# S5 chunk recurrence in two levels, and layer 0's readout with the states as stationary operand, in a two-layer hybrid diffusion block

## The chip, the core and the metric

One core of a Trainium2 chip runs the whole program in one launch. The metric is the device time of one execution in microseconds; the kernel is compared by the median of its runs. In the rows, PE is TensorE (matmul), PEld its weight loads, DVE is VectorE, ACT is ScalarE, POOL is GpSimd, SP is the engine whose queue issues most DMAs. L652 is line 652 of the kernel before.

## The reference

Two layers over 512 latent tokens and 256 context tokens, width 1024. Each layer normalizes, projects the input into three branches (a bidirectional S5 state space model, a gated DeltaNet, windowed attention), merges them by gates and adds an MLP. The change is in the S5 branch: for each of 32 groups, 64 complex states and two directions,

```python
s_re, s_im = associative_scan(complex_affine_combine, (a_re, a_im, bu_re, bu_im), reverse=reverse)
y = y + einsum('blgp,ghp->blgh', s_re, c_re) - einsum('blgp,ghp->blgh', s_im, c_im)
```

that is s[t] = a s[t-1] + B u[t], first over the context tokens and then over the latent ones from the state that the context left, forwards and backwards. The last layer has no context output.

## The kernel before

Tokens are cut into chunks of 8: 32 context chunks (NCC) and 64 latent ones (NCL), 96 in all (NCH). Within a chunk the S5 is a set of products with tables that depend on the weights alone; only the state at the chunks' borders needs a recurrence.

`s5_in` (L608) does two things. For each of 16 pairs of groups (pr), TensorE multiplies the chunk inputs u4 with a table om (L631) and ScalarE and VectorE copy the result into the state tile st, shifted by one chunk (L634 to L637). Then the recurrence runs over the chunks in place, both directions at once: 94 steps of four products and sums on VectorE (L652 to L655), each over 128 partitions x 64 elements (2 directions, real and imaginary, 16 pairs). Each step needs the one before.

`s5_out` (L659) reads the states out: for each pair a product with u4 (L678, L685) and four with the tables gm (L680, L690). In layer 0 (with_ctx) the tables are the stationary operand, 128 columns, and the 96 chunks move; the output has the right layout at once. In layer 1 the latent chunks' states are stationary, 64 columns, the table of 128 columns moves, two halves lie on different quarters of the array, and four transposes (L703) per quarter of the readout turn the result. Both write yt and then DRAM.

The program is written as Python generators; a scheduler puts the instructions of each engine into a fixed order when the program is built, and each engine runs its own order. Around the recurrence stand, in both layers, twelve convolutions of the DeltaNet inputs (`dn_conv`): a weight group is loaded (ws), split into a high and a low part (wh on ScalarE L227; wl on VectorE, or on GpSimd in these stretches, L228), TensorE multiplies (L178, into pg), ScalarE copies into cxp (L867), VectorE and GpSimd add the taps (L876, L880) and VectorE writes the result (L888). cxp, cac and ctp have two buffers each. The attention's k and q pass through the same buffers and a rotation (L731 to L734) and splits (L749, L775). In layer 0 the readout is drawn in between attention units (L797 to L844), which take their transposes' PSUM from the same two banks (tag "s") as the readout; in layer 1 it precedes the DeltaNet's main part, whose gaps are filled with the gates' products (L178).

```python
    for k in range(1, NCH - 1):
        v.tensor_tensor(t1, view(k - 1), A12[:, 0], op=OP.mult)
        v.tensor_tensor(t2, view(k - 1, True), A12[:, 1], op=OP.mult)
        v.tensor_tensor(t1, t1, view(k), op=OP.add)
        v.tensor_tensor(view(k), t1, t2, op=OP.add)
```

Of the kernel before, what the change touches and what calls it, by code (L numbers as in the profile page):

```python
# [607 lines left out]
def s5_in(g, l, pool, u4):  # L608
    nc = g.nc
    st = g.st = pool.tile([128, 2, 2, 16, SLOT], F32, name="st")  # L610
    nc.gpsimd.memset(st[:, 0, :, :, 0], 0.0)
    nc.gpsimd.memset(st[:, 1, :, :, NCC - 1], 0.0)
    A12 = pool.tile([128, 2, 2, 2, 16], F32, name="A12")
    v = nc.vector
    for d in range(2):
        s = slice(l * 32 + d * 16, l * 32 + d * 16 + 16)
        ar, ai = g.apw[:, 0, s, 7], g.apw[:, 1, s, 7]
        v.tensor_copy(A12[:, 0, d, 0], ar)
        v.tensor_copy(A12[:, 0, d, 1], ar)
        v.tensor_scalar(A12[:, 1, d, 0], ai, -1.0, None, op0=OP.mult)  # L620
        v.tensor_copy(A12[:, 1, d, 1], ai)
    tb = g.tb[l]
    for pr in range(16):
# [14 lines left out]
    RS = 16 * SLOT  # L638
    DS = 2 * RS

    order = list(range(NCC - 1, -1, -1)) + list(range(NCH - 1, NCC, -1))
    rpos = [(c - 1) % NCH for c in order]

    def view(k, swap=False):
        f, r = k + 1, rpos[k]
        dd = [[DS + r - f, 2], [-RS if swap else RS, 2], [SLOT, 16]]
        return raw(st, f + (RS if swap else 0), dd)

    for k in range(1, NCH - 1):
        t1 = pool.tile([128, 2, 2, 16], F32, name="rt1", tag="rt1", bufs=2)  # L650
        t2 = pool.tile([128, 2, 2, 16], F32, name="rt2", tag="rt2", bufs=2)
# [7 lines left out]
def s5_out(g, l, pool, upool, u4, with_ctx, yd):  # L659
# [3 lines left out]
    n = NCH - c0  # L663
    for m in range(4):
        mt = pool.tile([128, 8, 128], F32, name="mt", tag="mt", bufs=1 if with_ctx else 2)
        dma(g, QT[l]).dma_start(mt, g.hd[l][m].rearrange("t c g x -> (t c) g x"))
        py = [pm(g, "s") for _ in range(2 if with_ctx else 1)]
        for j in range(4):
            pr = 4 * m + j
            if pr % SG[l] == 0:  # L670
                gms = pool.tile([128, SG[l], 512], F32, name="gm", tag="tbr", bufs=SB[l])
                dma(g, QT[l]).dma_start(gms, tb[pr:pr + SG[l], :, TB_G:TB_G + 512].rearrange("j p c -> p j c"))
            gm = gms[:, pr % SG[l]]
            if with_ctx:
# [7 lines left out]
            else:  # L682
                o = [py[0][64 * h:64 * h + 64, 128 * j:128 * j + 128] for h in range(2)]
                for h in range(2):
                    nc.tensor.matmul(o[h], lhsT=u4[:, 2 * pr + h, c0:], rhs=mt[:, 2 * j + h, :], start=True, stop=False,  # L685
                                     tile_position=(0, 64 * h))
                for k in range(4):
                    for h in range(2):
                        pp = slice(64 * h, 64 * h + 64)
                        nc.tensor.matmul(o[h], lhsT=st[pp, k // 2, k % 2, pr, c0:], rhs=gm[pp, k * 128:k * 128 + 128],  # L690
                                         start=False, stop=k == 3, tile_position=(64 * h, 64 * h))
            yield
        y = upool.tile([128, 4, 2, NCH], F32, name="yt", tag="uy", bufs=2)
# [1134 lines left out]
```

## Time and profile before

| what | us |
|---|---|
| median of the 3 runs | 2945.91 (2945.82 to 2971.23) |
| the profiled execution | 2966.88 |
| its span in the trace | 2965.1 |
| TensorE busy | 2729.9 (92% of the span) |
| VectorE busy | 1669.2 (56%) |
| ScalarE busy | 908.1 (31%) |
| GpSimd busy | 558.1 (19%) |

The profile is of one execution, so its numbers belong to 2966.88 us, not to the median. The shares are averages over stages with different bounds; a stage's own row says what holds it. A granted clock of 1.00 is 2.4 GHz; TensorE's other level is 0.50, 1.2 GHz, and a number between them is a mean over time.

### The profile page before, as it was taken

To read this page: it belongs to the slowest core of one execution; us is meant where nothing else is said; L and a number is where in the kernel's file an instruction comes from. 1 tells how busy PE (TensorE), PEld (TensorE's weight loads), DVE (VectorE), ACT (ScalarE), POOL (GpSimd) and SP (SyncE) were. 2 spreads that over 40 slices of the span, in tenths; PEclk is the share of its full clock that TensorE was granted. 3 is DMA by queue.
4 is the path that set the end of the run, shared out by engine and by line. 5 is a ranking of instruction groups with operands and counts; after the bars stand their busy time and mean duration, and the time that the engine had idled before them with its cause. 6 is when DMAs were issued, how large, how long until landed. Compare 5 with 4: busy or idle time off the path is not lost. (4 is left out here: it accounts for less than half of the span.)

```text
span 2965.1 us, 46215 instructions
## 1 busy us (share of the span) xinstructions
PE 2729.9 (92%) x17908; PEld 2193.9 (74%) x17908; DVE 1669.2 (56%) x4335; ACT 908.1 (31%) x1643; POOL 558.1 (19%) x733
## 2 busy tenths in 40 slices
PE   5698899999999999999999999758997999999998
PEld 1585578878677877787778878646775768789997
DVE  7839985245336647747432324997456368444443
ACT  2243344232222323223121324332342234323322
POOL 4643331030213300000000001442253133000000
PEclk8799899699999999999999999879997999999999
DMA  6564322236116433535341225223432226233231
GB/s 226 160 219 161 136 80 79 69 123 174 42 38 204 137 109 108 161 125 151 120 133 67 67 84 176 73 66 120 138 102 76 93 84 208 77 99 99 87 100 65
DMA packets 206620, 343.63 MB, mean 116 GB/s; under 512 B 89280, under 2 KB 121152, under 8 KB 206400
## 3 DMA queue, kind: packets, MB, share of 16 engines
q1 hardware_dynamic: 171712, 297.56, 31.4%
q0 software_dynamic: 9600, 36.71, 3.7%
q10 hardware_dynamic: 25088, 6.40, 1.0%
q8 instruction: 141, 2.31, 0.3%
q14 instruction: 79, 0.65, 0.1%
HBM read 269.04 MB, written 68.16 MB: 114 GB/s over the span
## 5 line engine op out<-in xcount | busy, mean ns | idle before, releaser
L228 DVE TENSOR_TENSOR wl<-ws,wh 128x1024 fp32r<-128x1024 f32 x234 | 293.5, 1256 | 341.0 <-ACT wh L227 306.8
L227 ACT CAST wh<-ws 128x1024 fp32r<-128x1024 f32 x272 | 284.8, 1049 | 606.4 <-PE pg L178 477.9
L178 PE MATMUL pg<-hhil,wh 128*128 128x512 f32 x720 | 296.4, 412 | 51.5 <-ACT cxp L867 35.9
L178 PE MATMUL pg<-hlol,wh 128*128 128x512 f32 x720 | 294.0, 409 | 0.4 <-DVE hlol L350 0.4
L178 PE MATMUL pg<-hhil,wl 128*128 128x512 f32 x720 | 293.1, 407 | 0.1
L178 PE MATMUL pg<-hh,wh 128*128 128x512 f32 (+1 forms) x832 | 285.6, 344 | 3.1 <-DVE x L1657 2.8
L178 PE MATMUL pg<-hlo,wh 128*128 128x512 f32 (+1 forms) x800 | 280.9, 351 | 6.2 <-DVE hlo L350 6.2
L178 PE MATMUL pg<-hhi,wh 128*128 128x512 f32 (+1 forms) x800 | 281.4, 352 | 5.1 <-ACT cxp L867 5.1
L178 PE MATMUL pg<-hh,wl 128*128 128x512 f32 (+1 forms) x832 | 284.0, 342 | 1.0 <-DVE wl L228 1.0
L178 PE MATMUL pg<-hl,wh 128*128 128x512 f32 (+1 forms) x832 | 284.7, 343 | 0.0
L178 PE MATMUL pg<-hhi,wl 128*128 128x512 f32 (+1 forms) x800 | 279.4, 349 | 0.0
L178 PEld LDWEIGHTS pg<-hhil,wh 128*128 128x128 f32 x720 | 139.5, 194 | 96.7 <-ACT cxp L867 37.4
L1657 DVE SCALAR_TENSOR_TENSOR x<-pg,modv,x 128x512 f32<-128x512 f32 (+1 forms) x104 | 64.9, 626 | 259.5 <-PE pg L178 259.3
L178 PEld LDWEIGHTS pg<-hlo,wh 128*128 128x128 f32 x800 | 154.7, 193 | 37.4 <-issue 14.0
L178 PEld LDWEIGHTS pg<-hh,wh 128*128 128x128 f32 x832 | 157.3, 189 | 33.8 <-issue 12.1
L178 PEld LDWEIGHTS pg<-hhi,wh 128*128 128x128 f32 x800 | 155.2, 194 | 31.6 <-issue 9.0
L178 PEld LDWEIGHTS pg<-hl,wh 128*128 128x128 f32 x832 | 157.4, 189 | 27.9 <-issue 10.6
L178 PEld LDWEIGHTS pg<-hhi,wl 128*128 128x128 f32 x800 | 154.6, 193 | 29.3 <-issue 11.7
L178 PEld LDWEIGHTS pg<-hh,wl 128*128 128x128 f32 x832 | 157.3, 189 | 22.8 <-issue 2.9
L178 PEld LDWEIGHTS pg<-hlol,wh 128*128 128x128 f32 x720 | 139.4, 194 | 36.8 <-issue 6.6
L178 PEld LDWEIGHTS pg<-hhil,wl 128*128 128x128 f32 x720 | 139.2, 193 | 36.9 <-issue 5.6
L307 POOL TENSOR_TENSOR nr<-nv,cneg 128x2 f32<-128x2 f32 (+1 forms) x10 | 9.3, 933 | 645.5 <-ACT nsq L290 350.2
(421 smaller groups left out, 6115.8 us busy)
## 6 DMA issues: line engine op xcount, KB each, us to landing
ws<-in_wt SPq DMA_DIRECT2D x272, 512.0 KB, 3.6
wa<-in_wmod SPq DMA_DIRECT2D x96, 512.0 KB, 4.3
gtd<-gr POOLq DMA_DIRECT2D x24, 384.0 KB, 2.9
tg<-gtd POOLq DMA_DIRECT2D x24, 384.0 KB, 3.5
tb<-tC SPq DMA_DIRECT2D x64, 128.0 KB, 2.3
cvd<-ctp SPq DMA_DIRECT2D x20, 384.0 KB, 2.6
gtd<-gr POOLq DMA_DIRECT2D x24, 256.0 KB, 2.6
tg<-gtd POOLq DMA_DIRECT2D x24, 256.0 KB, 3.1
```

What stands on the lines that cost most here:

```text
L178: g.nc.tensor.matmul(ps, lhsT=wt[:, a], rhs=x(k), start=i == 0, stop=i == n - 1)
L227: nc.scalar.copy(hi, s)
L228: g.wle.tensor_tensor(lo, s, hi.bitcast(F32), op=OP.subtract)
L307: nc.gpsimd.tensor_tensor(r[:, :m], v[:, :m], g.cneg.to_broadcast([128, m]), op=OP.pow)
L1657: g.nc.vector.scalar_tensor_tensor(g.x[:, m, sl], acc, g.modv[:, l, 40 + m, p.r:p.r + 1], g.x[:, m, sl], op0=OP.mult, op1=OP.add)
```

## The change

The recurrence is done in two levels. The 96 chunk positions of a direction become 12 groups of 8. First each group runs its own recurrence from zero, all 12 groups in one instruction: 7 positions, for each direction four instructions over 2 x 16 x 12 = 384 elements. Then the 11 later groups' last positions are corrected one after the other with the eighth power of a (the step over a whole group): 11 steps of four instructions over 64 elements, as the old steps. Then the corrected group ends are spread over the 7 inner positions of the next group with the powers a to a^7: 12 times four instructions over 6 x 7 x 11 = 462 or 4 x 7 x 11 = 308 elements. The powers are worked out ahead by 18 short products. The direction that runs backwards now lies in the state tile in one line from end to start, so that the positions of a group lie 8 apart in memory; the extra copy L637 goes away and ScalarE's copies take its element.

The readout of layer 0 takes layer 1's form for the latent chunks, and for the context chunks the same with stationary pieces of 32 columns: two pairs at a time, four column places. Both results pass through a copy (yc), four and two transposes, and copies into yt. The scratch of the recurrence lies in buffers of other tiles (tags mt, tbr, uy), and the attention output ao has one buffer (AOB) in place of two.

```diff
-    nc.gpsimd.memset(st[:, 1, :, :, NCC - 1], 0.0)
+    nc.gpsimd.memset(st[:, :, 1, :, NCH - 1], 0.0)
+    pw = g.p5a[1].tile([128, 8 * NCH], F32, name="apw8", tag="uy", bufs=2)
+    tp = pool.tile([128, 1024], F32, name="scr", tag="mt", bufs=2 if l else 1)
+    for n in (1, 2, 4):
...
+        for k in range(4):
+            v.tensor_tensor(t[k], a[k // 2], b[k % 2], op=OP.mult)
+        v.tensor_tensor(o[0], t[0], t[3], op=OP.subtract)
+        v.tensor_tensor(o[1], t[1], t[2], op=OP.add)
...
-        nc.scalar.copy(st[:, 1, :, pr, :NCC - 1], p3[:, 1, :, 1:NCC])
-        nc.scalar.copy(st[:, 1, :, pr, NCC:NCH - 1], p3[:, 1, :, NCC + 1:])
-        nc.vector.tensor_copy(st[:, 1, :, pr, NCH - 1:], p3[:, 1, :, 0:1])
+        nc.scalar.copy(st[:, :, 1, pr, NCL - 1:NCH - 1], p3[:, 1, :, :NCC])
+        nc.scalar.copy(st[:, :, 1, pr, :NCL - 1], p3[:, 1, :, NCC + 1:])
+    tp.append([pool.tile([128, SG[l] * 512], F32, name="scs", tag="tbr", bufs=SB[l]) for _ in range(2)])
...
-    for k in range(1, NCH - 1):
-        v.tensor_tensor(t1, view(k - 1), A12[:, 0], op=OP.mult)
-        v.tensor_tensor(t2, view(k - 1, True), A12[:, 1], op=OP.mult)
-        v.tensor_tensor(t1, t1, view(k), op=OP.add)
-        v.tensor_tensor(view(k), t1, t2, op=OP.add)
+    NI, NS = 8, NCH // 8
+    def mac(t, a, sw, ar, ai, o):
+        v.tensor_tensor(t[0], a, ar, op=OP.mult)
+        v.tensor_tensor(t[1], sw, ai, op=OP.mult)
+        v.tensor_tensor(t[0], t[0], o, op=OP.add)
+        v.tensor_tensor(o, t[0], t[1], op=OP.add)
+    for i in range(1, NI):
+        for d in range(2):
+            vw = lambda f, sw=False: raw(st, at(d, f) + (RS if sw else 0), [[-RS if sw else RS, 2], [SLOT, 16], [-NI if d else NI, NS]])
+            mac(tmp(d, 2, 16, NS), vw(i - 1), vw(i - 1, True), raw(pw, 9 * 16 * d, [[0, 2], [9, 16], [0, NS]]),
+                raw(pw, 9 * (32 + 16 * d) + 8, [[-8, 2], [9, 16], [0, NS]]), vw(i))
+    for s_ in range(1, NS):
...
+        mac(tmp(s_ % 2, 2, 2, 16), vw(p), vw(p, 1), raw(pw, 7, [[0, 2], [9 * 16, 2], [9, 16]]), nim, vw(f))
+    for q, nq in ((0, 6), (6, 6), (12, 4)):
+        for r in range(2):
+            for d in range(2):
+                c = [raw(st, x * RS + at(d, NI - 1) + b_, [[SLOT, nq], [0, NA], [sg * NI, NS - 1]]) for x in (r, 1 - r)]
+                o = raw(st, r * RS + at(d, NI) + b_, [[SLOT, nq], [sg, NA], [sg * NI, NS - 1]])
...
+                v.tensor_tensor(t[0], c[0], a8[0], op=OP.mult)
+                v.tensor_tensor(t[1], c[1], a8[1], op=OP.mult)
+                v.tensor_tensor(t[0], t[0], o, op=OP.add)
+                v.tensor_tensor(o, t[0], t[1], op=OP.add if r else OP.subtract)
...
-                    nc.tensor.matmul(o, lhsT=mt[:, 2 * j + h, :], rhs=u4[:, 2 * pr + h, c0:], start=True, stop=False)
-                    for k in range(4):
-                        nc.tensor.matmul(o, lhsT=gm[pp, k * 128:k * 128 + 128], rhs=st[pp, k // 2, k % 2, pr, c0:],
-                                         start=False, stop=k == 3)
+                        nc.tensor.matmul(o(jj, h), lhsT=u4[:, 2 * (4 * m + jj) + h, cs], rhs=mt[:, 2 * jj + h, :], start=True,
+                                         stop=False, tile_position=(0, col(jj, h)))
+                            nc.tensor.matmul(o(jj, h), lhsT=st[pp, k % 2, k // 2, 4 * m + jj, rs if k // 2 else cs],
+                                             rhs=gms[jj][pp, k * 128:k * 128 + 128], start=False, stop=k == 3,
+                                             tile_position=(64 * h, col(jj, h)))
+            unit(lambda jj, h: pl[64 * h:64 * h + 64, 128 * jj:128 * jj + 128], slice(NCC, NCH), [j], lambda jj, h: 64 * h)
+            if with_ctx and j % 2:
+                cp = lambda jj, h: 64 * h + 32 * (jj % 2)
+                unit(lambda jj, h: pc[cp(jj, h):cp(jj, h) + 32, 64 * (j - 1):64 * (j - 1) + 128], slice(0, NCC), [j - 1, j], cp)
...
+AOB = 1
```

VectorE in layer 1, at the end of the recurrence, before: L652 to L655 are its steps, L731 to L734 a q rotation, L775 a q split, L228 a weight's low part.

```order
L731 STREAM_SHUFFLE ash<-arf 128x512
L775 TENSOR_TENSOR arf<-arf,aq 64x512
L652 TENSOR_TENSOR rt_17872<-st,A_17093 128x64
L653 TENSOR_TENSOR rt_17873<-st,A_17093 128x64
L775 TENSOR_TENSOR arf<-arf,aq 64x512
L733 TENSOR_TENSOR ash<-ash,rt 128x512
L654 TENSOR_TENSOR rt_17872<-rt_17872,st 128x64
L734 TENSOR_TENSOR arf<-arf,ash 128x512
L655 TENSOR_TENSOR st<-rt_17872,rt_17873 128x2x32
L652 TENSOR_TENSOR rt_17878<-st,A_17093 128x64
```

The same place after the change, in the changed kernel's own lines: L683 to L686 are the spreading, L913 and L925 the last convolution (L876 and L888 before), L768 to L771 the k rotation.

```order
L685 TENSOR_TENSOR scr<-scr,st 128x308
L685 TENSOR_TENSOR scs<-scs,st 128x308
L686 TENSOR_TENSOR st<-scr 128x4x7x11
L686 TENSOR_TENSOR st<-scs 128x4x7x11
L913 SCALAR_TENSOR_TENSOR cac<-cxp,sm,cac 128x512 x2
L925 SCALAR_TENSOR_TENSOR ctp<-cxp,cac 128x4x64 x4
L768 STREAM_SHUFFLE ash<-arf 128x512
L770 TENSOR_TENSOR ash<-ash,rt 128x512
L771 TENSOR_TENSOR arf<-arf,ash 128x512
L786 TENSOR_TENSOR akl<-arf,akh 64x768 x2
```

The recurrence was woven through the q rotations; now its last instructions stand ahead of the last convolution's end and of all rotations.

TensorE in layer 1 at the start of the readout, before: L178 are gate products, L913 the last of the small DeltaNet input products, L690 and L685 the readout.

```order
L178 MATMUL pg<-hhil,wl 128x512
L913 MATMUL pm<-ca,cxp 64x16 x4
L690 MATMUL ps<-gm,st 64x128 x8
L685 MATMUL ps<-mt,u_16838 64x128 x2
L690 MATMUL ps<-gm,st 64x128 x8
L685 MATMUL ps<-mt,u_16838 64x128 x2
L690 MATMUL ps<-gm,st 64x128 x8
L685 MATMUL ps<-mt,u_16838 64x128 x2
```

After the change, where the first quarter of the readout starts: L717 and L711 are the readout, the L178 above it the k product over the context tokens (hloc, hhic), the L178 below it the v product.

```order
L178 MATMUL pg<-hhic,wh 128x256
L178 MATMUL pg<-hloc,wh 128x256
L178 MATMUL pg<-hhic,wl 128x256
L717 MATMUL ps<-gm,st 64x128 x8
L711 MATMUL ps<-mt,u_16636 64x128 x2
L717 MATMUL ps<-gm,st 64x128 x8
L711 MATMUL ps<-mt,u_16636 64x128 x2
L717 MATMUL ps<-gm,st 64x128 x8
L711 MATMUL ps<-mt,u_16636 64x128 x2
L717 MATMUL ps<-gm,st 64x128 x8
L178 MATMUL pg<-hhil,wh 128x512
L178 MATMUL pg<-hlol,wh 128x512
```

The readout began behind the products for k, v, q and the small inputs; now its first quarter stands between k and v, and v and the four q products come behind it.

## Rows read from the trace of the kernel before

**Rows 1.** The page, part 2: two of its rows, forty equal slices.

```profile
DVE  7839985245336647747432324997456368444443
...
PEclk8799899699999999999999999879997999999999
```

**Rows 2.** Stages: length, then PE, PEld, DVE, ACT, POOL busy (count), PEclk, DMA share, GB/s.

```profile
214.00:395.00 181.00, 147.92 (x761) 103.63 (x758) 175.74 (x473) 61.52 (x89) 70.53 (x62) 0.91 0.41 145
490.00:588.00 98.00, 95.09 (x582) 81.44 (x578) 28.79 (x105) 23.05 (x62) 8.89 (x27) 0.69 0.23 74
1855.00:2047.00 192.00, 132.89 (x601) 105.73 (x599) 186.08 (x456) 63.98 (x90) 80.07 (x67) 0.83 0.22 70
2047.00:2087.00 40.00, 40.00 (x410) 31.32 (x411) 11.65 (x31) 10.61 (x20) 3.59 (x4) 1.00 0.58 177
```

**Rows 3.** What TensorE waited for in 1855 to 2047 us: total, times, longest.

```profile
PE pg L178 <- ACT cxp L867: 37.8, 6, 11.5
```

**Rows 4.** The recurrence's four instructions (tile rt) in the two stretches: DVE busy, PEclk, DMA.

```profile
214.00:395.00 181.00, 143.63 (x378) 0.91 0.41 145
1855.00:2047.00 192.00, 148.91 (x377) 0.83 0.22 70
```

**Rows 5.** VectorE in order of time, one step of the recurrence: start, length.

```profile
1864.93 0.27 DVE L652 TENSOR_TENSOR rt<-st,A 128x64 f32<-128x64 f32 x1
1865.12 0.27 DVE L653 TENSOR_TENSOR rt<-st,A 128x64 f32<-128x64 f32 x1
1865.30 0.27 DVE L654 TENSOR_TENSOR rt<-rt,st 128x64 f32<-128x64 f32 x1
1865.60 0.28 DVE L655 TENSOR_TENSOR st<-rt,rt 128x64 f32<-128x64 f32 x1
1865.91 2.28 DVE L652 TENSOR_TENSOR rt<-st,A 128x64 f32<-128x64 f32 x1
```

**Rows 6.** GpSimd in order of time, the same place.

```profile
1865.72 2.40 POOL L228 TENSOR_TENSOR wl<-ws,wh 128x1024 fp32r<-128x1024 f32 x1 [1.96 <-ACT wh L227]
```

**Rows 7.** VectorE in order of time: two products of 64 and one of 512.

```profile
30.25 0.26 DVE L480 TENSOR_TENSOR f<-apw,s5v 128x64 f32<-128x64 f32 x1
...
30.61 0.22 DVE L479 TENSOR_TENSOR f<-am,s5v 128x64 f32<-128x64 f32 x1
...
2442.96 1.09 DVE L1594 SCALAR_TENSOR_TENSOR zz<-yq,yi 128x512 f32<-128x512 f32 x1
```

**Rows 8.** VectorE's groups by line and form: count, busy, mean ns.

```profile
L1699 DVE TENSOR_TENSOR rl<-rl 128x512 f32<-128x512 f32 x32 | 21.9, 684 | 0.0
```

**Rows 9.** VectorE's groups by line in 1855 to 2047 us: the rotations.

```profile
L731 DVE STREAM_SHUFFLE ash<-arf 128x512 f32<-128x512 f32 x5 | 3.7, 737 | 0.0
L733 DVE TENSOR_TENSOR ash<-ash,rt 128x512 f32<-128x512 f32 x5 | 3.5, 693 | 0.0
L734 DVE TENSOR_TENSOR arf<-arf,ash 128x512 f32<-128x512 f32 x5 | 3.4, 685 | 0.0
```

**Rows 10.** One group of 24 products of L178, 512 wide: PE and PEld busy, PEclk.

```profile
1862.10:1867.90 5.80, 5.78 (x26) 4.34 (x24) 1.00 0.00 0
```

**Rows 11.** TensorE's groups by line, 490 to 588 us (layer 0).

```profile
L680 PE MATMUL ps<-st,gm 64*128 64x96 f32 x256 | 44.8, 370 | 0.0
L678 PE MATMUL ps<-u,mt 128*128 128x96 f32 x64 | 16.2, 367 | 0.0
```

**Rows 12.** TensorE's groups by line, 2047 to 2087 us (layer 1).

```profile
L690 PE MATMUL ps<-gm,st 64*64 64x128 f32 x256 | 17.4, 275 | 0.0
...
L685 PE MATMUL ps<-mt,u 128*64 128x128 f32 x60 | 6.6, 298 | 0.0
...
L703 PE MATMUL ps<-ca,yc 128*128 128x128 f32 x12 | 1.8, 272 | 0.0
```

**Rows 13.** The tile ao: its copy, and the landing of its writes.

```profile
L844 ACT COPY ao<-ps x40: 238/265/288, 408.7 to 2296.0; 128x128 f32<-128x128 f32 x40
...
DMA to landing us min/median/max: 1.8/1.9/6.0
```

More of the change, by code (lines that the diff above doesn't have):

```diff
@@ new lines, in s5_in, with tmp @@
+        nc.scalar.copy(st[:, :, 0, pr, 1:], p3[:, 0, :, :NCH - 1])
+        nc.scalar.copy(st[:, :, 1, pr, NCL - 1:NCH - 1], p3[:, 1, :, :NCC])
+        nc.scalar.copy(st[:, :, 1, pr, :NCL - 1], p3[:, 1, :, NCC + 1:])
+    tp.append([pool.tile([128, SG[l] * 512], F32, name="scs", tag="tbr", bufs=SB[l]) for _ in range(2)])
+    def tmp(d, *sh):
+        dims = " ".join(f"d{i}" for i in range(len(sh)))
+        return [t[:, :math.prod(sh)].rearrange(f"p ({dims}) -> p {dims}", **{f"d{i}": x for i, x in enumerate(sh)}) for t in tp[d]]
@@ L666, in s5_out @@
         dma(g, QT[l]).dma_start(mt, g.hd[l][m].rearrange("t c g x -> (t c) g x"))
-        py = [pm(g, "s") for _ in range(2 if with_ctx else 1)]
+        pl = pm(g, "s")
+        pc = pm(g, "s") if with_ctx else None
+        gms = [None] * 4
         for j in range(4):
@@ new lines, in s5_out, with unit @@
+                blk = pool.tile([128, SG[l], 512], F32, name="gm", tag="tbr", bufs=SB[l])
+                dma(g, QT[l]).dma_start(blk, tb[pr:pr + SG[l], :, TB_G:TB_G + 512].rearrange("j p c -> p j c"))
+            gms[j] = blk[:, pr % SG[l]]
+            def unit(o, cs, js, col):
+                rs = slice(0, NCL) if cs.start else slice(NCL, NCH)
+                for jj in js:
+                    for h in range(2):
+                        nc.tensor.matmul(o(jj, h), lhsT=u4[:, 2 * (4 * m + jj) + h, cs], rhs=mt[:, 2 * jj + h, :], start=True,
+                                         stop=False, tile_position=(0, col(jj, h)))
+                for k in range(4):
+                    for jj in js:
+                        for h in range(2):
+                            pp = slice(64 * h, 64 * h + 64)
+                            nc.tensor.matmul(o(jj, h), lhsT=st[pp, k % 2, k // 2, 4 * m + jj, rs if k // 2 else cs],
+                                             rhs=gms[jj][pp, k * 128:k * 128 + 128], start=False, stop=k == 3,
+                                             tile_position=(64 * h, col(jj, h)))
@@ L705, in s5_out @@
-        dma(g, QS).dma_start(yd[m][:, :, c0:], y.rearrange("p j h c -> p (j h) c")[:, :, :n])
+        yc = pool.tile([128, 512], F32, name="yc", tag="yc", bufs=1)
+        nc.scalar.copy(yc, pl)
+        pt = pm(g, "s")
+        for j in range(4):
+            nc.tensor.transpose(pt[:, 128 * j:128 * j + 128], yc[:, 128 * j:128 * j + 128], g.ident)
+        nc.vector.tensor_copy(y[:, :, :, NCC:], pt.rearrange("p (j h c) -> p j h c", j=4, h=2))
+        if with_ctx:
+            yx = pool.tile([128, 512], F32, name="yc", tag="yc", bufs=1)[:, :256]
+            nc.vector.tensor_copy(yx, pc[:, :256])
+            px = pm(g, "s")
+            for j in range(2):
+                nc.tensor.transpose(px[:, 128 * j:128 * j + 128], yx[:, 128 * j:128 * j + 128], g.ident)
+            for j in range(2):
+                nc.scalar.copy(y[:, 2 * j:2 * j + 2, :, :NCC].rearrange("p a h c -> p h a c"),
+                               px[:, 128 * j:128 * j + 128].rearrange("p (h a c) -> p h a c", h=2, a=2))
```

80 lines of the change are left out of this document (28 added, 52 removed).

## The prediction

> **What bounds the kernel now.** I read the page's slices first, then a table of stages, then the waits of the stages in which TensorE does not run flat out. The page says that TensorE is the bound nearly everywhere; the places for this change are the two where VectorE's digit is 9 and the granted clock drops, slices 4 and 5 and slices 26 and 27 [rows 1]. By stage [rows 2]: from 214 to 395 us (layer 0) VectorE is busy for 175.7 of 181 us, from 1855 to 2047 us (layer 1) for 186.1 of 192. TensorE is busy for 147.9 and 132.9 there, at a granted clock of 0.91 and 0.83, so a part of this time it runs at 1.2 GHz. It waits for ScalarE's copy into cxp, 37.8 us in layer 1 [rows 3], and that waits for a cxp buffer that VectorE has not finished with. Both stretches are therefore as long as VectorE's queue. The recurrence is most of that queue: 143.6 and 148.9 us [rows 4]. The third place is the readout of layer 0, 490 to 588 us, where TensorE is busy for 95.1 of 98 us at 0.69. The readout of layer 1, 2047 to 2087 us, runs at 1.00 [rows 2].
>
> **The recurrence, removed.** It has 94 steps of four instructions in each layer. An undisturbed step takes from one L652 to the next, 1864.93 to 1865.91, 0.98 us [rows 5]: 94 x 0.98 = 92.1 us. The rest of layer 1's 148.9 us, 57 us, is standing: the L652 at 1865.91 takes 2.28 us where its like takes 0.27 [rows 5], and a GpSimd instruction of 2.40 us has started just before it [rows 6].
>
> **The recurrence, added.** Per layer there are 56 instructions of 384 elements (7 positions, 2 directions, 4 each), 44 of 64 (11 group ends, 4 each), and for the spreading 32 of 462 and 16 of 308. 148 follow where 376 stood, but with 1.8 times the elements. What an element costs decides. In nearly every one of them one operand steps by 8 floats. The trace shows such operands: L480 reads apw at that step, 64 elements, 0.26 us, while L479, all contiguous, takes 0.22; L1594 writes zz at that step, 512 elements, 1.09 us [rows 7], where a contiguous product of 512 takes 0.684 [rows 8]. So the strided price is (1.09 - 0.26) / 448 = 1.85 ns an element, the contiguous one (0.684 - 0.22) / 448 = 1.04. Starts lie 0.08 closer than an instruction is long (0.19 apart at 0.27, [rows 5]). Strided, 384 elements cost 0.26 + 320 x 0.00185 - 0.08 = 0.77 us, 462 cost 0.92, 308 cost 0.63. Sum: 56 x 0.77 = 43.1; the group ends are 11 old steps, 10.8; 32 x 0.92 + 16 x 0.63 = 39.5; and in 26 groups the last instruction waits for the one before it (0.30 instead of 0.19, [rows 5]), 2.9. That is 96.3 against 92.1: +4 per layer, +8 in all, because the stretch is VectorE's.
>
> Bounds: at the contiguous price 384, 462 and 308 cost 0.47, 0.55 and 0.39, the sum is 26.3 + 10.8 + 23.8 + 2.9 = 64, which is -28 per layer; at twice it (2.08 ns) 47 + 10.8 + 43 + 2.9 = 104, +12 per layer. The long reads at a step of 8 have no row of their own. I take the strided price, since the one long row is a written operand and the short rows show a read to cost extra too.
>
> The Trainium skill (SBUF — State Buffer, section Specifications) says that a 16-byte line has to be hit at least twice for full bandwidth and that each change of line costs, which speaks against steps of 32 bytes whether read or written. It would put the long reads at the strided price too; the trace agrees for what it shows, 0.26 against 0.22 and 1.09 against 0.684, and has no long read.
>
> **The standing of 57 us** I leave as it is: the L652 stood for 2.28 us beside an instruction of 2.40, so its length follows GpSimd's work (80.1 us in the stretch, [rows 2]), which the change does not touch, and not the number of VectorE's instructions. The Trainium skill (SBUF — State Buffer, section Who interferes with whom) says that a VectorE instruction with two SBUF inputs and a reading GpSimd instruction shut each other out for a whole instruction; by that the standing stays, too, and the trace agrees with this one pair. The other reading is the second rival.
>
> **Small parts.** The powers of a are 23 short instructions of 0.2 us, 4.6 us; they stand ahead of the convolutions, in slices 3 and 25 where VectorE's digits are 3 and 4 [rows 1], and cost nothing; without that cover 4.6 a layer. The 16 copies of L637 go into ScalarE's copies, in the same slices: nothing. One attention output buffer in place of two: a copy to ao is followed by a write that lands after 1.9 us [rows 13], and between two copies a whole unit of products, softmax and transposes stands; nothing. If half of the 40 copies waited 1 us, 20 us of ScalarE, which is busy for 23 of 98 us there [rows 2].
>
> **The order in layer 1.** Before, the recurrence was woven through to the end of the q rotations, and TensorE did v and the four q products while VectorE was the bound. Now the spreading ends before the k rotation, a quarter of the readout stands before v, and v and q come behind. VectorE's stretch loses the five rotations, 10.6 us in three lines [rows 9], and with the k and q splits and GpSimd's products beside them I take 20. TensorE's part behind it grows by five groups of 24 products at 5.78 us [rows 10] and half a one for v's context, 31.8, less the readout quarter that now lies ahead (a quarter of 26.8, below), 6.7: +25. So +5; from -15 (TensorE still gets its products in beside) to +15 (VectorE saves only its 10.6).
>
> **The readout of layer 0.** Before: 44.8 + 16.2 = 61.0 us of TensorE [rows 11], at 0.69. Its latent half becomes what layer 1 has: 17.4 + 6.6 x 64/60 + 1.8 x 16/12 = 26.8 us at full clock [rows 12]. The context half has as many products again (8 units of 20), on stationary pieces of 32 columns with four column places in turn. They cost as much as the latent ones, 24.4, if two run beside each other, or 12.2 if four do, and 1.2 for eight transposes. Together 40 to 52, about 46 at 2.4 GHz. I take 51, some of it at 1.2 GHz: -10. Bounds: 40 at full clock, -21; all of it at 1.2 GHz, 92, +31. The extra copies of each quarter lie beside attention units, with VectorE busy for 29 and ScalarE for 23 of 98 us [rows 2]. A pair of gm tiles is now held until its context unit is done, with three buffers; a late fourth would stop TensorE, within that upper bound.
>
> **Sum.** +8 + 5 - 10 = +3 us on the profiled execution's 2966.9. That execution lies 21 us above the median of the runs, 2945.9; the difference carries over, 2949 us. A measurement here tells about 1%, 29 us, from no change.
>
> **Rivals.**
> 1. *Steps of 8 are free in long instructions* (only L1594 says otherwise, and that is a write with three operands). Then -56 + 5 - 10 = -61: 2885 us. Both stretches leave room for it: TensorE is idle for 33 and 59 us in them, beside the low clock [rows 2]. Chance 0.22.
> 2. *The standing goes by the number of instructions.* 57 x 148/376 = 22 us a layer, -35 each: 8 - 70 + 5 - 10 = -67, 2879 us. Against it: rows 5 and 6. Chance 0.08. The rule of the Trainium skill named above (SBUF — State Buffer, section Who interferes with whom) speaks against it as well.
> 3. *Slower: the clock in layer 0's readout.* The clock fell there under products that use half of the rows [rows 2, 11]; the new ones use a quarter of the array each and the context ones an eighth. If all of it runs at 1.2 GHz, 92 instead of 61: 8 + 5 + 31 = +44, 2990 us. It becomes slower by over 1% from 77 us of readout on. For it: 0.69 in this stretch, with no wide products between. Against it: 1.00 in layer 1 with the same latent products, though wide ones stand between those. Chance 0.20.
>
> The forecast holds 0.50. Rivals 1 and 2 and a little of the forecast's lower end (0.02) make faster by over 1%: 0.32. Rival 3 and the upper end (0.03) make slower: 0.23. Within 1%: 0.45. The likeliest case alone spans 2925 to 2975; with the others, 2872 to 2990.
>
> **What would show it.** Instructions of 384 elements at about 0.85 us and of 462 at about 1.0 (0.55 and 0.63 would make rival 1 right); VectorE still over 95% busy in both stretches, each as long as before within 10 us or, in layer 1, shorter by 15 with more TensorE work behind it; layer 0's readout at 51 us or less and a granted clock above 0.69 there. Stretches shorter by 25 us or more, or a readout of over 75 us, would make the forecast wrong.

## The result, and the profile after

The changed kernel takes 3001.04 us (median of 4 runs, 3000.08 to 3003.14), the kernel before beside it 2955.1 (4 runs): a ratio of 1.0135, 95% interval 1.0090 to 1.0181. It is slower; the forecast was 2949 and no change, with 2990 as the upper end. Profile against profile it is 3003.14 against 2966.88, +36.3 us.

The two page rows of the changed kernel that answer to [rows 1]:

```profile
DVE  7849955336336646757432324995457368444443
...
PEclk8798899999999999999999999779997999999999
```

The same slices carry the 9 of VectorE. The clock's digits in them fall from 98 to 88 in layer 0 (slices 4 and 5) and from 87 to 77 in layer 1 (slices 26 and 27). More is to be seen if each stretch is cut where the last convolution ends. Stages of the kernel before, from the recurrence's first instruction to the convolutions' last, in layer 0 and in layer 1, and the readout of layer 0 between the two neighbouring L178 products (columns as in [rows 2]):

```profile
214.10:370.40 156.30, 130.57 (x681) 89.06 (x678) 151.86 (x403) 55.66 (x77) 61.77 (x55) 0.91 0.44 156
1853.70:1993.50 139.80, 92.73 (x408) 75.16 (x407) 135.92 (x327) 49.61 (x69) 64.07 (x56) 0.82 0.21 68
477.70:589.30 111.60, 106.09 (x681) 89.84 (x679) 40.26 (x147) 31.29 (x83) 12.27 (x39) 0.72 0.23 75
```

The same three of the changed kernel, and the time from there to the end of layer 1's readout:

```profile
213.50:392.50 179.00, 130.55 (x645) 85.99 (x644) 164.69 (x225) 54.86 (x77) 92.41 (x54) 0.86 0.41 142
1870.10:2044.10 174.00, 98.03 (x450) 79.52 (x450) 164.60 (x201) 50.85 (x72) 83.58 (x59) 0.76 0.19 63
499.20:610.90 111.70, 88.89 (x1028) 65.03 (x1027) 43.41 (x151) 33.88 (x93) 11.39 (x39) 0.89 0.23 78
2044.10:2120.10 76.00, 76.00 (x569) 58.53 (x566) 33.05 (x61) 25.87 (x43) 18.16 (x14) 1.00 0.47 136
```

TensorE is busy for the same time up to the end of layer 0's convolutions, 130.57 and 130.55 us (645 products for 681, at a clock of 0.86 for 0.91), but within 179.0 us where it had 156.3: that is 22.7 us, and the products behind the readout start 21.6 us later (610.9 for 589.3). In layer 1 the convolutions take 174.0 for 139.8, 34.2 more. Behind them the readout's last transposes end after 76.0 us; before, they ended at 2092.0, 98.5 us behind 1993.5. That leaves 34.2 - 22.5 = 11.7 us from the start of the recurrence on. The whole kernel loses 36.3 - 21.6 = 14.7 behind layer 0's readout: these 11.7, and 7.9 behind layer 1's readout (881.0 for 873.1), where TensorE is busy for 6.7 us more, less 5.2 that the stretch between the two layers gives back (1259.2 for 1264.4). Kernel before, from the recurrence's end to the last transposes and from there to the end:

```profile
2045.40:2092.00 46.60, 46.60 (x441) 36.45 (x440) 14.81 (x35) 13.16 (x23) 4.59 (x8) 1.00 0.52 161
2092.00:2965.10 873.10, 822.98 (x5846) 686.92 (x5844) 437.04 (x961) 280.83 (x498) 143.46 (x225) 0.96 0.32 102
```

Changed kernel, from the last transposes to the end:

```profile
2120.10:3001.10 881.00, 829.72 (x5885) 694.62 (x5883) 438.19 (x967) 282.76 (x501) 145.18 (x227) 0.97 0.34 102
```

How much of the recurrence stands ahead of the convolutions' end is seen from the tile st on VectorE. Kernel before, ahead of and behind that end, in layer 0 and in layer 1 (length, VectorE busy with the recurrence, clock):

```profile
214.10:370.40 156.30, 125.35 (x328) 0.91 0.44 156
370.40:395.00 24.60, 14.71 (x50) 0.86 0.26 75
1853.70:1993.50 139.80, 112.73 (x276) 0.82 0.21 68
1993.50:2045.40 51.90, 34.84 (x102) 0.87 0.27 79
```

Changed kernel:

```profile
213.50:392.50 179.00, 127.01 (x148) 0.86 0.41 142
1870.10:2044.10 174.00, 138.42 (x148) 0.76 0.19 63
```

The new recurrence costs VectorE less than the old one: 127.0 for 125.4 + 14.7 = 140.1 us, and 138.4 for 147.6. But before, 14.7 and 34.8 us of it stood behind the last convolution; now all of it stands ahead. In layer 0 the amount ahead hardly grew, 127.0 for 125.4; there the convolutions in between lost their place. The last VectorE instructions of the ninth of the twelve, before and changed:

```profile
317.76 0.49 DVE L888 SCALAR_TENSOR_TENSOR ctp<-cxp,cac 128x128 f32<-128x128 f32 x2
```

```profile
354.94 0.51 DVE L925 SCALAR_TENSOR_TENSOR ctp<-cxp,cac 128x128 f32<-128x128 f32 x2
```

It ends 37.2 us later, and in this stretch VectorE itself now stands idle for 179.0 - 164.7 = 14.3 us, where it was 4.4: it waits for ScalarE's steps of the convolutions. What TensorE waited for in 1870.1 to 2044.1 (37.8 us in [rows 3]):

```profile
PE pg L178 <- ACT cxp L904: 71.2, 8, 16.6
```

### The profile page after: what moved, and what is told of

It reads as the page before. It is cut to its first block, busy times and chain, and to the rows that moved or that the text cites. A ratio compares the mean times of both kernels' runs of the same rounds, so it can differ in the third digit from the quotient of the medians.

```text
span 3001.1 us, 46419 instructions
## 1 busy us (share of the span) xinstructions
PE 2712.5 (90%) x18252; PEld 2171.6 (72%) x18252; DVE 1672.4 (56%) x3881; ACT 910.7 (30%) x1651; POOL 605.5 (20%) x733
## 4 chain that ended last, share of the span: by engine, by line
PE 73%; DVE 17%; issue 3%; DMA 3%; ACT 1%; POOL 1%; SPq 1%; ACTq 0%; DVEq 0%; POOLq 0%
PE pg L178 51%; PE pg L1598 4%; PE ps L869 1%; PE ps L717 1%; PE ps L878 1%; PE ps L251 1%; DVE st L661 1%; PE pm L292 1%; PE pm L1220 1%; PE pm L1251 1%; DVE cac L913 1%; PE pm L1229 1%; DVE scs L658 1%; PE pg L1648 1%; PE ps L1266 1%
## 5 line engine op out<-in xcount | busy, mean ns | idle before, releaser
L228 DVE TENSOR_TENSOR wl<-ws,wh 128x1024 fp32r<-128x1024 f32 x234 | 293.1, 1254 | 355.0 <-ACT wh L227 320.9
L178 PE MATMUL pg<-hhil,wh 128*128 128x512 f32 x720 | 295.1, 410 | 63.1 <-ACT cxp L904 63.1
L178 PE MATMUL pg<-hhi,wh 128*128 128x512 f32 (+1 forms) x800 | 282.9, 354 | 21.6 <-ACT cxp L904 19.0
L178 PE MATMUL pg<-hlol,wh 128*128 128x512 f32 x720 | 292.3, 406 | 1.1 <-DVE hlol L350 1.1
L178 PE MATMUL pg<-hhil,wl 128*128 128x512 f32 x720 | 292.9, 407 | 0.0
L178 PE MATMUL pg<-hh,wh 128*128 128x512 f32 (+1 forms) x832 | 286.2, 345 | 3.4 <-DVE x L1695 2.9
L178 PE MATMUL pg<-hlo,wh 128*128 128x512 f32 (+1 forms) x800 | 282.1, 353 | 6.2 <-DVE hlo L350 6.2
L178 PE MATMUL pg<-hh,wl 128*128 128x512 f32 (+1 forms) x832 | 284.7, 343 | 1.0 <-DVE wl L228 1.0
L178 PE MATMUL pg<-hl,wh 128*128 128x512 f32 (+1 forms) x832 | 285.4, 344 | 0.0
L178 PE MATMUL pg<-hhi,wl 128*128 128x512 f32 (+1 forms) x800 | 280.2, 350 | 0.0
L178 PEld LDWEIGHTS pg<-hhil,wh 128*128 128x128 f32 x720 | 138.6, 193 | 107.9 <-ACT cxp L904 65.2
L178 PEld LDWEIGHTS pg<-hhi,wh 128*128 128x128 f32 x800 | 155.9, 195 | 51.3 <-ACT cxp L904 20.6
L178 PEld LDWEIGHTS pg<-hh,wh 128*128 128x128 f32 x832 | 158.1, 190 | 34.2 <-issue 12.1
L178 PEld LDWEIGHTS pg<-hlo,wh 128*128 128x128 f32 x800 | 155.6, 194 | 35.0 <-issue 11.3
L178 PEld LDWEIGHTS pg<-hl,wh 128*128 128x128 f32 x832 | 158.0, 190 | 27.9 <-issue 10.6
L178 PEld LDWEIGHTS pg<-hhi,wl 128*128 128x128 f32 x800 | 155.2, 194 | 31.1 <-issue 13.6
L178 PEld LDWEIGHTS pg<-hh,wl 128*128 128x128 f32 x832 | 158.1, 190 | 22.9 <-issue 2.9
L178 PEld LDWEIGHTS pg<-hhil,wl 128*128 128x128 f32 x720 | 138.7, 193 | 37.4 <-issue 6.3
L178 PEld LDWEIGHTS pg<-hlol,wh 128*128 128x128 f32 x720 | 138.8, 193 | 36.0 <-issue 5.6
L917 POOL TENSOR_TENSOR cac<-cac,ctp 128x772 f32<-128x772 f32 (+1 forms) x47 | 126.2, 2685 | 95.1 <-DVE cac L913 55.4
```

The source lines that it names most:

```text
L178: g.nc.tensor.matmul(ps, lhsT=wt[:, a], rhs=x(k), start=i == 0, stop=i == n - 1)
L228: g.wle.tensor_tensor(lo, s, hi.bitcast(F32), op=OP.subtract)
L917: nc.gpsimd.tensor_tensor(acc[:, :w], acc[:, :w], tap[:, :w], op=OP.add)
```

## The experiments

Three explanations run through the expectations. *Price*: the steps of 8 make the new VectorE instructions long. *Order*: the recurrence now stands ahead of convolutions that TensorE waits for. *Shut-out*: VectorE and GpSimd keep each other from starting.

The times are medians; the kernel before ran beside them with 2964.9 (first four), 2962.3 (next four), 2966.8 (next four) and 2966.1 us (last two). The ratios, with 95% intervals, are to those runs; they differ from the quotient of the medians by up to 0.3%. Each diff is an excerpt.

**e1, the readout alone.** `s5_in` of the kernel before, `s5_out` of the changed one and its single buffer for ao (A12 in a tile of tag uy, for room).

```diff
-    A12 = pool.tile([128, 2, 2, 2, 16], F32, name="A12")
+    A12 = g.p5a[1].tile([128, 8 * NCH], F32, name="A12", tag="uy", bufs=2)
...
-        py = [pm(g, "s") for _ in range(2 if with_ctx else 1)]
+        pl = pm(g, "s")
+        pc = pm(g, "s") if with_ctx else None
...
```

> The old recurrence with the new readout of layer 0 (and one attention output buffer). The traces so far put the whole loss ahead of 400 us and between 1855 and 2060 us, where no readout of layer 0 stands: the time is that of the kernel before within 10 us. The step of the prediction (a readout shorter by 10 us) gives 10 us less than before. If the readout had a part in the loss, 10 to 30 us more than before. In the stretch of layer 0's readout TensorE should be busy for about 80 us where it was busy for 95, and the stretch about as long (95 to 100 us), because attention's softmax sets its pace.

2966.5 us, ratio 1.0026 (1.0003 to 1.0050). The readout gains nothing; by the interval it costs 1 to 15 us. Its stage in e1, to be held against 477.70:589.30 above:

```profile
477.10:590.30 113.20, 90.72 (x1029) 66.98 (x1027) 43.43 (x151) 33.73 (x91) 11.58 (x39) 0.88 0.21 76
```

TensorE is busy for 15.4 us less and the clock is up from 0.72 to 0.88, yet the stage is 1.6 us longer. The readout's own products and transposes take 45.2 us in it:

```profile
L687 PE MATMUL ps<-gm,st 64*64 64x128 f32 (+1 forms) x512 | 29.2, 284 | 1.0 <-DMA gm<-tb 1.0
L681 PE MATMUL ps<-mt,u 128*32 128x128 f32 (+1 forms) x128 | 10.9, 308 | 0.0
L701 PE MATMUL ps<-ca,yc 128*128 128x128 f32 x16 | 3.2, 338 | 0.4 <-ACT ao L851 0.4
L708 PE MATMUL ps<-ca,yc 128*128 128x128 f32 x8 | 1.9, 323 | 4.8 <-DVE yc L705 3.6 <-DVE aM L826 1.2
```

Some of what TensorE waits for there in e1 (L839 and L848 are attention's transposes and products with v, L804 the scores, L708 the new context transposes):

```profile
PE ps L839 <- ACT aPT L844: 4.1, 6, 0.7
PE ps L708 <- DVE yc L705: 3.6, 3, 1.2
PE pm L804 <- DVE aM L815: 3.5, 5, 0.7
PE ps L839 <- DVE aPT L842: 3.1, 4, 0.8
```

TensorE stood idle for 5.5 us before (111.6 - 106.1) and stands for 22.5 now: by all rows of this view 16.1 ahead of attention's own products and 6.2 ahead of the readout's. So the work saved turned into waiting.

**e2, the recurrence alone.** `s5_out` of the kernel before.

```diff
-st[pp, k // 2, k % 2, pr, c0:]
+st[pp, k % 2, k // 2, pr, c0:]
```

> The new recurrence with the old readout of layer 0; the readout takes the backward states of layer 0 and 1 in another order of chunks, so its values are not the reference's, with the same instructions. If the loss is the recurrence's: 40 to 55 us over before, the convolutions of layer 0 end near 392 us as in the changed kernel (370 before) and those of layer 1 50 us later than before. If the two parts of the change only lose together: within 15 us of before.

2995.4 us, ratio 1.0133 (1.0084 to 1.0182): +30 us by the medians and 39 by the ratio, a little under the 40 expected. Most of the loss is the recurrence's.

**e3, no steps of 8.** Positions and groups exchanged in every operand.

```diff
-[[-RS if sw else RS, 2], [SLOT, 16], [-NI if d else NI, NS]]
+[[-RS if sw else RS, 2], [SLOT, 16], [-1 if d else 1, NS]]
```

> The changed kernel with each operand of the group steps and of the spreading moved to neighbouring elements (positions of a group 12 apart, groups side by side), so that no operand steps by 8 floats; the states that come out are not the reference's. Number, size and order of VectorE's instructions stay. Theory price (the steps of 8 cost the time): 384 elements fall from 0.87 to about 0.5 us, 462 from 1.02 to about 0.6, some 33 us of VectorE less per layer, and the time goes below before, 2900 to 2945. Theory order (what counts is how much VectorE time stands ahead of the convolutions): nearly the same, 2915 to 2955, with the convolutions of layer 0 ending at about 365 us. Theory shut-out (GpSimd gets in only between VectorE's instructions, and these leave no gap): GpSimd's additions of the convolutions still take over 110 us in all (126 in the changed kernel) and the time stays above 2975.

2937.5 us, ratio 0.9915 (0.9882 to 0.9947). Undisturbed instructions of 384 elements in VectorE's order of time, changed kernel, then e3:

```profile
254.82 0.88 DVE L658 TENSOR_TENSOR scs<-st,apw 128x384 f32<-128x384 f32 x1
255.58 0.88 DVE L659 TENSOR_TENSOR scs<-st,apw 128x384 f32<-128x384 f32 x1
```

```profile
238.17 0.55 DVE L658 TENSOR_TENSOR scs<-st,apw 128x384 f32<-128x384 f32 x1
238.63 0.55 DVE L659 TENSOR_TENSOR scs<-st,apw 128x384 f32<-128x384 f32 x1
```

Against the changed kernel 64 us are gone. The same order with shorter instructions also shortens what stands ahead of the convolutions, so price and order both expected this.

**e4, the old order.** The recurrence is traced in pieces between the convolutions; each piece is held behind the convolution's last VectorE instruction.

```diff
         dn_conv(g, l, pc, i, pl, pcx, put, dve)
+        with tc.issue_after(g.cvl):
+            weave(RW[l][g.rk])
+        g.rk += 1
```

> The changed kernel with the same instructions in another order on VectorE: after each convolution's last instruction only as large a share of the recurrence follows as stood there in the kernel before (0, 8, 16, 26, 37, 46, 54, 56, 68, 78, 87% of it behind the second to the twelfth convolution of layer 0; 76% at the twelfth of layer 1), the rest behind the last. Theory order: the convolutions end within 6 us of before (370 us in layer 0, against 392 in the changed kernel), the recurrence ends later (near 390 us), and the time is 2940 to 2965. Theory price (VectorE's work is the bound, wherever it stands): 2985 to 3005, as the changed kernel. Theory shut-out: GpSimd's additions stay as long as in the changed kernel (2.2 us median, single ones over 6 us) and the time over 2980.

2991.4 us, ratio 1.0111 (1.0054 to 1.0168): it gives back 10 us only. The order's expectation is missed, and the time lies where price had it (2985 to 3005). Layers 0 and 1 up to the convolutions' end, and layer 1 from there to the recurrence's end:

```profile
212.30:379.40 167.10, 134.66 (x699) 92.62 (x698) 162.06 (x212) 56.42 (x79) 77.38 (x56) 0.90 0.42 145
1860.70:2008.50 147.80, 93.62 (x416) 76.21 (x415) 143.00 (x169) 50.45 (x71) 75.57 (x58) 0.80 0.19 64
2008.50:2048.50 40.00, 27.75 (x122) 22.49 (x121) 39.94 (x45) 6.65 (x9) 11.83 (x5) 0.88 0.14 43
```

Layer 0 gets back half (167.1 us, between 156.3 and 179.0), and layer 1's convolutions most (147.8, between 139.8 and 174.0). But there the rest of the recurrence now fills VectorE behind them, and TensorE has done 93.6 + 27.8 = 121.4 us of work when it ends, where before it had done 132.9 [rows 2]. So layer 1 gained nothing in the end. The order did its part all the same: TensorE's wait for cxp up to the convolutions' end of layer 1 is back at what it was before (37.8, [rows 3]), from 71.2:

```profile
PE pg L178 <- ACT cxp L908: 38.9, 6, 11.8
```

But in nearly the old order the new kernel still costs 26 us against the kernel before.

**e5 and e6, one pair of scratch tiles**, in the changed order and in the woven one.

```diff
-for t in tp[d]]
+for t in tp[0]]
```

> The changed kernel with one pair of scratch tiles for both directions, where it has two: each step's four instructions now stand behind one another, and the last of them needs the one just ahead of it. The order otherwise is nearly that of the changed kernel (100% of layer 0's recurrence ahead of the last three convolutions, 98% in layer 1). Theory shut-out (GpSimd gets in only where a VectorE instruction has to wait for the one before it): GpSimd's additions fall from 126 us in all to under 100 and none stands over 4 us (11.7 now); the time falls by 10 to 25 us, to 2975 to 2990, although VectorE itself pays some 0.1 us for each such wait, 5 to 7 us a layer. Theory order alone: no gain beyond 5 us.

> The woven order of e4 with the single pair of scratch tiles of e5. e4 left TensorE 8 us (layer 0) and 7 us (layer 1) more idle in the stretches than the kernel before, while GpSimd's additions were 10 and 7.5 us longer. If that rest is the shut-out: additions back to 46 and 37 us, the time 10 to 15 us below e4, 2972 to 2982. If the rest is VectorE's price: 2990 to 3005, 0 to 12 above e4, because of the waits added.

The reason for both is this GpSimd instruction of the changed kernel, in order of time, and the VectorE instructions that passed meanwhile (eight more follow, the last at 331.10):

```profile
322.10 11.73 POOL L917 TENSOR_TENSOR cac<-cac,ctp 128x772 f32<-128x772 f32 x1 [7.11 <-DVE md L259]
```

```profile
321.94 1.04 DVE L685 TENSOR_TENSOR scr<-scr,st 128x462 f32<-128x462 f32 x1
322.84 1.10 DVE L685 TENSOR_TENSOR scs<-scs,st 128x462 f32<-128x462 f32 x1
323.81 0.21 DVE L261 TENSOR_TENSOR modv<-md,sm 128x8 f32<-128x8 f32 x1
323.89 1.13 DVE L686 TENSOR_TENSOR st<-scr 128x462 f32<-128x462 f32 x1
...
331.10 1.06 DVE L685 TENSOR_TENSOR scs<-scs,st 128x462 f32<-128x462 f32 x1
```

The 47 additions (shortest, median, longest in ns) before, changed, and in e5:

```profile
L880 POOL TENSOR_TENSOR cac<-cac,ctp x47: 1259/1848/2047, 190.4 to 1984.3; 128x772 f32<-128x772 f32 x39, 128x512 f32<-128x512 f32 x8
```

```profile
L917 POOL TENSOR_TENSOR cac<-cac,ctp x47: 1257/2223/11732, 191.3 to 2041.4; 128x772 f32<-128x772 f32 x39, 128x512 f32<-128x512 f32 x8
```

```profile
L917 POOL TENSOR_TENSOR cac<-cac,ctp x47: 1260/2155/4957, 191.0 to 2022.9; 128x772 f32<-128x772 f32 x39, 128x512 f32<-128x512 f32 x8
```

e5: 2982.1 us, ratio 1.0073 (1.0052 to 1.0093), 19 us below the changed kernel, the time that shut-out expected. Its signs just miss: the additions take 101 us in all (126 changed), the longest 4.96. And e5 doesn't show the shut-out alone, for its order moved too: 37% of the recurrence stands ahead of the sixth convolution's end in layer 0 where the changed kernel has 55%, and 79% for 89% at the ninth. Nor do the convolutions of layer 0 end any earlier for the shorter additions (393.8, changed 392.5):

```profile
392.62 1.16 DVE L925 SCALAR_TENSOR_TENSOR ctp<-cxp,cac 128x256 f32<-128x256 f32 x4
```

e6: 2990.7, ratio 1.0110 (1.0068 to 1.0151), no better than e4: missed. Its additions fell only from e4's 100.7 to 98.0 us. The two repairs don't add up.

**e7, the woven order without GpSimd's taps.**

```diff
+CDV0 = [5] * 12
+CDV1 = [5] * 12
```

> The woven order of e4 with all four taps of every convolution on VectorE: GpSimd adds no tap any more and ScalarE makes no product for it. VectorE has 47 more instructions of about 1.0 us, 44 us in all. Theory shut-out (each GpSimd addition holds VectorE for some 1.55 us and itself waits): VectorE gets back about 47 x 1.55 = 73 us, the convolutions of layer 0 end before 372 us (379 in e4) and the time is 2955 to 2985. If the additions cost VectorE little: 20 to 45 us slower than e4, 3010 to 3035.

2963.1 us, ratio 1.0003 (0.9981 to 1.0025), 28 us below e4, as expected.

**e8, pairs inside.** The state tile turned: positions outside, the 16 pairs inside, so the long steps go and the computation stays.

```diff
-    st = g.st = pool.tile([128, 2, 2, 16, SLOT], F32, name="st")
+    st = g.st = pool.tile([128, 2, 2, NCH, 16], F32, name="st")
```

> The changed kernel with the state tile turned, positions outside and the 16 pairs inside, so that every operand of the recurrence runs over 16 neighbouring elements; the spreading is cut by groups (8 x 448 and 4 x 336 elements per direction and part) in place of pairs; ScalarE's copies into the state tile and the readout's stationary operand now step by 16 floats. The order on VectorE is that of the changed kernel. Theory price: the instructions fall to 0.5 and 0.6 us as in e3 and the time is that of e3 within 10 us, 2930 to 2950, if the stepping copies and weight loads are hidden. If the stepping loads are not hidden, the readout of layer 1 grows (40 us now) and the time is 2950 to 2990. If runs of 16 elements cost as much as single ones: 2990 to 3005.

2934.4 us, ratio 0.9911 (0.9879 to 0.9943): the price theory's number. An instruction of 448 elements takes 0.61 us, as little as one without any step (462 elements took 0.63 in e3):

```profile
327.03 0.61 DVE L686 TENSOR_TENSOR st<-scs 128x448 f32<-128x448 f32 x1
```

**e9 and e10, e8 with one scratch pair, and e8 without GpSimd's taps.** The edits of e5 and e7.

> The turned state tile of e8 with the single pair of scratch tiles of e5. In e8 VectorE stands idle for 17.6 and 16.4 us of the stretches, waiting for convolutions whose GpSimd additions take 127 us in all. Theory shut-out: additions under 100 us, VectorE's idle time under 10 us a layer, and since VectorE now has room for its own waits the time falls by 3 to 15 us against e8 (2934), to 2920 to 2931. If GpSimd's lateness is not what VectorE waits for: 2934 to 2945.

> The turned state tile of e8 with all taps on VectorE (47 more instructions of 1.0 us there, none of GpSimd's additions). Theory shut-out: VectorE pays 44 us and gets back about 73 us of standing and most of its idle 34 us; TensorE is then the bound in more of both stretches: 2900 to 2930. If the additions cost little beside the shorter instructions: 2940 to 2965.

e9: 2937.6 us, ratio 0.9914 (0.9883 to 0.9945): missed. Its longest addition is 3.80 us (10.79 in e8) and the time is the same: either the long additions did not hold e8, or VectorE's own waits, which one pair of scratch tiles adds, cost as much. Its order moved as e5's did. e10: 2899.6, ratio 0.9791 (0.9752 to 0.9831), just under the lower end, and the fastest that leaves nothing out.

**e11 and e12, the additions left out** of the changed kernel and of the kernel before.

```diff
-            nc.gpsimd.tensor_tensor(acc[:, :w], acc[:, :w], tap[:, :w], op=OP.add)
```

> The changed kernel with GpSimd's 47 additions of convolution taps left out, so those taps are missing from the result; ScalarE still makes their products. To be compared with e12. Theory shut-out: without the additions the two kernels lie closer, the changed one 0 to 15 us above e12 instead of 36. Theory price and order without GpSimd: the distance stays, 25 to 40 us.

> The kernel before with the same 47 additions left out. VectorE stands for about 1.55 us beside each, 73 us in all over both layers, a part of it behind the last convolution: 2890 to 2930.

e11: 2936.4 us, ratio 0.9912 (0.9884 to 0.9940); e12: 2899.5, ratio 0.9789 (0.9753 to 0.9826). Without any addition to shut out, the two are still 37 us apart, so the shut-out of the additions is not the main cause.

**e13, the old instructions in the new order.** The last instructions of each convolution wait for the share of the recurrence that stands there in the changed kernel.

```diff
+    n_ = round(len(g.steps) * RW[l][g.rk] / 100)
+    with g.tc.issue_after(g.steps[n_ - 1]) if n_ else nullcontext():
```

> The kernel before with its own 94 steps in each layer, its own readout, and the order of the changed kernel on VectorE: the last instructions of each convolution are held until as large a share of the recurrence is through as in the changed kernel (0, 12, 32, 47, 53, 62, 78, 89, 100, 100, 100% at the second to the twelfth convolution of layer 0; 100% at the twelfth of layer 1, where before it was 87% and 73%). Theory order: no element and no stride has changed, and yet the time goes up as in the changed kernel, by 20 to 50 us, to 2985 to 3015; the convolutions end near 392 us in layer 0 (370 before). Theory price (what the two-level steps cost on VectorE): within 12 us of before.

2987.5 us, ratio 1.0071 (1.0044 to 1.0099), +21 us, in the range of the order's expectation; the convolutions of layer 0 end at 384.4, not near 392. The two stretches up to the convolutions' end:

```profile
211.70:384.40 172.70, 127.73 (x639) 85.75 (x636) 155.28 (x453) 54.81 (x75) 61.96 (x55) 0.86 0.40 141
1847.90:2013.70 165.80, 94.02 (x464) 76.07 (x463) 153.80 (x430) 49.78 (x70) 61.84 (x56) 0.78 0.18 62
```

172.7 us for 156.3 and 165.8 for 139.8: the order alone lengthens both, by 16 and 26 us of the changed kernel's 23 and 34. In layer 0 GpSimd is at 62.0 and not at 92.4. The ninth convolution of layer 0 ends at 351.4 (318.3 before, 355.5 changed), and TensorE's wait for cxp in layer 1's stretch is that of the changed kernel:

```profile
351.10 0.28 DVE L892 SCALAR_TENSOR_TENSOR ctp<-cxp,cac 128x128 f32<-128x128 f32 x1
```

```profile
PE pg L178 <- ACT cxp L868: 70.0, 8, 18.0
```

**e14, the kernel before without GpSimd's taps.** The edit of e7.

> The kernel before with all taps of the convolutions on VectorE, as e10 has them, to tell how much of e10's gain belongs to the taps alone. e12 shows 65 us for the additions left out; 47 instructions of VectorE come back, 44 us, a part of them behind the stretch: 2925 to 2950. If the taps are neutral with the old recurrence, which fills VectorE longer: 2955 to 2975; then e10's gain needs the shorter recurrence.

2912.0 us, ratio 0.9815 (0.9787 to 0.9843): missed, faster than either range. So 54 of the 67 us of e10 belong to the taps, and the two-level recurrence with pairs inside adds 13, an amount that the two intervals don't tell apart.

## Why the prediction was wrong

**What failed: "it is +4 per layer ... because the stretch is VectorE's".** The stretches kept the length that the prediction gave them: up to VectorE's last instruction of the two, 179.0 us for 181 in layer 0, and 174.0 for 192 in layer 1 ("shorter by 15 with more TensorE work behind it"). But TensorE does not wait for the end of VectorE's queue. It waits for convolutions, which stand inside the queue, and their place in it moved. The prediction weighed the order for layer 1's v and q alone, +5, not for the convolutions, and for layer 0 it had no such term at all. The order by itself costs 21 us over both layers (e13). TensorE's wait for cxp in layer 1 goes with it: 37.8 us before, 71.2 in the changed kernel, 70.0 with the old instructions in the new order (e13), 38.9 with the new ones in nearly the old (e4). VectorE's order, shown with the change, had the sign of it: the last convolution's instructions behind the spreading's.

**What the order leaves open.** In nearly the old order the new kernel still costs 26 us by the medians (e4; 16 to 50 by the interval), where the sum had +8 for VectorE and -10 for the readout. So the step from VectorE's work to the time failed there too. The 21 and the 26 make 47, the whole change 40 by its ratio (27 to 53); whether they overlap can't be told. Nor is it shown how e4's 26 us divide between the long steps, the standing and the readout (1 to 15 us in e1). That the long steps have a large part is shown: in the changed order, without them, the kernel is 27 us faster than before (e3).

**The base was low.** The 2945.9 us were the median of three runs; beside the experiments the kernel before took 2962.3 to 2966.8.

**Layer 1's order term came out in its bounds.** It took VectorE's stretch as 20 us shorter and TensorE's part behind it as 25 longer. Measured: 191.7 - 174.0 = 17.7 shorter, and 76.0 for 46.6 (2045.4 to 2092.0), 29.4 longer, with TensorE busy for 76.0 of the 76.0. That is +11.7 instead of +5, within the bound of 15; another 7.9 (881.0 for 873.1) come behind it, where the prediction had no term.

**The price of one instruction was right.** Forecast 0.85 and 1.0 us for 384 and 462 elements, measured 0.88 and 1.04; without the steps 0.55 forecast and 0.55 measured. Rival 1 gave a free step 64 us against the forecast: e3 and e8 lie 64 and 67 us below the changed kernel. The rule of the Trainium skill (SBUF — State Buffer, section Specifications) that each change of a 16-byte line costs agrees with these long reads: 0.88 us at steps of 8 against 0.55 without.

**The standing.** It neither stayed nor went by the number of instructions (rival 2, 22 us a layer). Less the forecast price, 127.0 - 96.3 = 31 and 138.4 - 96.3 = 42 us of the new recurrence are standing; before it was 140.1 - 92.1 = 48 and 147.6 - 92.1 = 55 ([rows 4] also hold rotations, L733, which read a tile of the same name). Part of it moved to VectorE's other instructions, in layer 0's stretch 164.7 - 127.0 = 37.7 us for 151.9 - 125.4 = 26.5, and part to GpSimd, whose work there rose from 61.8 to 92.4.

That the two engines shut each other out for a whole instruction, as the Trainium skill says (SBUF — State Buffer, section Who interferes with whom), the trace bears out: an L652 took 2.28 us beside a GpSimd instruction of 2.40 [rows 5, 6], and the addition of 11.73 us ends at 333.83, 1.7 us behind the last of the VectorE instructions that ran meanwhile. It also shows that a waiting GpSimd instruction may be passed by eleven of VectorE's. What that costs, together with what the two-level steps cost, lies within the 9 us that e2 has over e13 (30 and 21; 18 by the ratios, whose intervals overlap); the two were not told apart.

**The readout of layer 0: -10 forecast, nothing gained.** The size of the work was right: TensorE is busy for 17.2 us less in the stage (106.1 to 88.9), and the readout itself takes 45.2 us in e1, forecast 51 and before 61.0. It failed on cover: the stage was taken as TensorE's because it was busy for 95.1 of 98 us, and the work saved came back as waiting (22.5 us in e1). Which wait sets the pace is not shown. Attention alone does not: in e13's profiled execution the old readout, beside the same attention, took 93.9 us, 18 less than the new one. **Rival 3** was wrong: the clock there went up, from 0.72 to 0.89. The powers and the copies cost nothing that the runs show. One output buffer was not tried apart; in the changed kernel's stage TensorE waits for the copy to ao for 2.6 us (L869 for L881), which it did not before.

## What to carry to other kernels

A stretch in which one engine is full is not yet the bound of another: look which of the full engine's instructions the other waits for, and count what stands ahead of each of these, before and after. An edit that makes a block of work shorter or freer of dependencies can let a fixed order put it ahead of work that was needed sooner. And lay the tile out so that the innermost run is contiguous: e3 shows 64 us for that alone, and e8, which also cuts the spreading into other pieces, 67.

## What was not expected of the hardware

- A GpSimd addition of 1.85 us stood for 11.73 us while VectorE ran instruction after instruction; in the kernel before, beside a chain of short dependent steps, none of the 47 took over 2.05.
- GpSimd's additions are dear beside a full VectorE: the 47 left out give 67 us (e12), and VectorE doing them itself still gives 54 (e14).
- Steps of 16 floats cost ScalarE's copies into st in e8 half as much again, while TensorE's products in the readout keep their time (0.269 and 0.272 us). Copies in the changed kernel and in e8:

```profile
L644 ACT COPY st<-ps x32: 290/318/342, 166.7 to 1869.8; 128x190 f32<-128x190 f32 x32
```

```profile
L644 ACT COPY st<-ps x32: 471/488/556, 166.7 to 1838.7; 128x190 f32<-128x190 f32 x32
```

- The old readout of layer 0 does not always get the same clock. In the profiled execution of e13, which has it unchanged, its stage ran at 0.91 and took 93.9 us, against 0.72 and 111.6:

```profile
491.40:585.30 93.90, 87.08 (x682) 72.89 (x680) 40.30 (x147) 31.28 (x83) 11.99 (x39) 0.91 0.26 90
```

That execution, 2972.96 us, is the shortest of e13's five (up to 2993.19). The kernel before spreads likewise, from 2941.9 us at a mean clock of 0.959 to 2982.4 at 0.942; the four runs of the changed kernel lie within 3.1 us.
